# Rotary embedding on one core: the wait for the last ten stores stands at the end of SyncE's program instead of ScalarE's

## The chip, the cores and the metric

The kernel runs on one core of a Trainium2 chip. The metric is the device time of an execution in microseconds (us). The profile's *span* is shorter than this time (160.6 against 162.42 us in the profiled run of before): it ends with the last instruction of the program.

## The reference

A float32 array of 16 x 512 x 1024 is seen as 16 heads of 64 values, and each head is rotated with tables of cosines and sines.

```python
x = x.reshape(batch, seq, num_heads, head_dim)          # 16, 512, 16, 64
x1, x2 = x[..., :half_dim], x[..., half_dim:]
rotated = np.concatenate([x1*cos - x2*sin, x1*sin + x2*cos], axis=-1)
```

The work is light. 33.5 MB have to be read and as many written.

## The kernel before

The kernel is five programs, one for each of five engines. They meet at semaphores, which an instruction or a transfer of one raises (`then_inc`) and another waits for (`wait_ge`). SyncE issues sixteen loads of 2 MB. VectorE multiplies by the cosines, GpSimd (now and then VectorE) multiplies the swapped halves by the signed sines, and the sum of the two is made by VectorE, or by TensorE with an identity matrix and a copy by ScalarE. ScalarE also issues the sixteen stores. Ten loads fit into the ring in SBUF. The last six loads reuse space, so each waits for one of the first six stores, which have semaphores of their own. The last ten stores share one, `sem_rest`.

```python
def on_sync(sp):
    for c in range(NC):                                  # NC = 16
        if c * R >= RING:                                # R = 4, RING = 40
            sp.wait_ge(sem_out[c - RING // R], 16)
        sp.dma_start(tile(c), xv[c]).then_inc(sem_in[c], 16)
        if c == 0:
            ...                                          # loads of the two tables
def on_scalar(ae):
    ...                                                  # copies of the sine table
    for u in range(NU):                                  # NU = 64
        c, r, k = where(u)
        if PE2[u]:
            ae.wait_ge(sem_e, n_pe[u])
            ae.activation(xs[:, k, :], t1_ps[:, u % NT1, :], COPY).then_inc(sem_a, 1)
        if r == R - 1:
            wait_added(ae, u)
            ae.dma_start(ov[c], tile(c)).then_inc(sem_out[c] if c < len(sem_out) else sem_rest, 16)
    ae.wait_ge(sem_rest, 16 * (NC - len(sem_out)))       # the wait in question: 160
```

The last line holds ScalarE until the last ten stores have landed: in before the last of them was issued at 152.16 us and landed at 160.516 us, and the wait ended at 160.555 us.

Of the kernel before, what the change touches and what calls it, by code (L numbers as in the profile page):

```python
# [6 lines left out]
def bass_split_heads_rope_kernel(  # L7
# [29 lines left out]
    NC = batch  # L37
    NU = batch * R

    def where(u):  # L40
        return u // R, u % R, u % RING
# [19 lines left out]
    with ExitStack() as stack:  # L61
# [9 lines left out]
        sem_out = [stack.enter_context(nc.semaphore(f"out{c}")) for c in range(NC - RING // R)]  # L71
        sem_rest = stack.enter_context(nc.semaphore("rest"))
# [21 lines left out]
        def tile(c):  # L94
            k = c * R % RING
            return x_sb[:, k:k + R].rearrange("p n h t d -> p (n h t d)")
# [7 lines left out]
        def wait_added(eng, u):  # L104

            if n_pe[u]:
                eng.wait_ge(sem_a, n_pe[u])
            if n_comb[u]:
                eng.wait_ge(sem_v, n_comb[u])
# [10 lines left out]
        def on_sync(sp):  # L120
            for c in range(NC):
                if c * R >= RING:
# [3 lines that stand above are left out]
                    for i, (table, sem) in enumerate(((cos, sem_cos), (sin, sem_sin))):  # L126
                        sp.dma_start(  # L127
                            stage[:, i, :], table.rearrange("(p r) d -> p (r d)", r=R)
                        ).then_inc(sem, 16)

        def on_scalar(ae):
            ae.wait_ge(sem_sin, 16)
            sv = stage[:, 1, :].rearrange("s (r d) -> s r d", d=HALF)
            ae.activation(s_sb[:, :, 0, :], sv, COPY, scale=-1.0)  # L134
            ae.activation(s_sb[:, :, 1, :], sv, COPY).then_inc(sem_s, 1)  # L135
            for u in range(NU):
# [4 lines that stand above are left out]
                if r == R - 1:  # L141
                    wait_added(ae, u)
                    ae.dma_start(ov[c], tile(c)).then_inc(sem_out[c] if c < len(sem_out) else sem_rest, 16)
            ae.wait_ge(sem_rest, 16 * (NC - len(sem_out)))

        def on_tensor(pe):
            pe.wait_ge(sem_z, 1)
# [49 lines left out]
        def on_vector(ve):  # L197
# [44 lines left out]
            for u in range(NU + LEAD):  # L242
                if u < NU:
                    mul(u)
                if u >= LEAD and not PE2[u - LEAD]:
                    comb(u - LEAD)

        on_sync(nc.sync)
        on_scalar(nc.scalar)
        on_gpsimd(nc.gpsimd)  # L250
        on_tensor(nc.tensor)
# [34 lines left out]
```

## Time and profile before

| before | |
|---|---|
| time, median of 3 runs | 162.3 us (162.14 to 162.39) |
| span of the profiled run, and its time | 160.6 us, 162.42 us |
| last load issued, landed | 84.7 us, 139.3 us |
| last store issued, landed | 152.16 us, 160.52 us |
| the last wait of ScalarE | 160.54 us, 17 ns |

Two lines of the page of before follow: the mean busy share of the 16 DMA engines in 40 equal slices, in tenths, and the rate in each slice.

```profile
DMA  5999999999999999999999999999999999999996
GB/s 147 400 453 425 441 420 400 416 445 416 445 433 416 445 412 447 433 416 441 418 445 433 420 433 429 441 433 420 433 429 437 437 420 437 425 437 441 412 441 286
```

Only the first and the last slice have room. The transfers bound the span, and the stretches of the table view say the same; after the range and its length it gives busy us and number of instructions for PE, PEld, DVE, ACT and POOL, then the granted clock, the DMA share and the rate.

```profile
10.00:50.00 40.00, 20.20 (x28) 6.69 (x28) 36.83 (x33) 6.14 (x6) 40.00 (x18) 0.67 1.01 428
85.00:130.00 45.00, 26.20 (x31) 8.21 (x31) 40.78 (x36) 8.19 (x8) 38.24 (x18) 0.57 1.01 431
156.00:160.60 4.60, 0.00 (x0) 0.00 (x0) 0.00 (x0) 0.00 (x0) 0.00 (x0) 0.50 0.69 296
```

The end, from the view in order of time (start, duration, engine and line), and ScalarE's wait, from the view of its source line:

```profile
151.10 1.02 ACT L140 ACTIVATE x_sb<-t_ps 128x1024 f32<-128x1024 f32 x1 [5.03 <-PE t_ps L164]
152.16 0.34 ACTq L143 DMA_DIRECT2D out_dram<-x_sb  x1
...
L144 ACTq EVENT_SEMAPHORE  x1: 17/17/17, 160.5 to 160.5; - x1
```

After the last copy and the last store's issue no engine computes for 8 us. The wait's record is 17 ns long and begins at 160.538 us, after the last landing at 160.516 us; it holds none of the time from 152.16 us on. A beginner may take the 8 us in front of it for its cost. They are data under way: 360 to 492 GB/s in each microsecond from 152 to 159 us.

### The profile page before, as it was taken

The numbers are of one execution on the slowest core, as the hardware profiler recorded it, in microseconds if no ns is written. First come the engines' busy times: TensorE is split into PE (matmuls) and PEld (weight loads), VectorE is DVE, ScalarE is ACT, GpSimd is POOL, SyncE is SP. The second block draws the span as 40 slices with busy tenths as digits, with TensorE's granted clock in tenths as the row PEclk, the third lists the DMA queues.
The fourth block names the chain that finished last, engine by engine and source line by source line (L and its number), as shares of the span: only waits on it lengthen the run. The fifth ranks groups of instructions, "written<-read, shape, count | busy, mean of one in ns | idle before, by whom it ended". The sixth has DMA issues, their size and how long they took to land.

```text
span 160.6 us, 607 instructions
## 1 busy us (share of the span) xinstructions
PE 84.1 (52%) x102; PEld 26.1 (16%) x102; DVE 131.5 (82%) x116; ACT 26.4 (16%) x27; POOL 130.3 (81%) x62
## 2 busy tenths in 40 slices
PE   6004907363635853864853764764675672684600
PEld 1002301210120220220221120221121121121100
DVE  0089399999999889996999799997999699996800
ACT  3010312022202112112102102202202202202200
POOL 1069999999999999999999993998939989399000
PEclk9955795569655685555675555675555675555775
DMA  5999999999999999999999999999999999999996
GB/s 147 400 453 425 441 420 400 416 445 416 445 433 416 445 412 447 433 416 441 418 445 433 420 433 429 441 433 420 433 429 437 437 420 437 425 437 441 412 441 286
DMA packets 4898, 67.26 MB, mean 419 GB/s; under 512 B 544, under 2 KB 800, under 8 KB 800
## 3 DMA queue, kind: packets, MB, share of 16 engines
q1 hardware_dynamic: 2592, 33.69, 49.9%
q10 hardware_dynamic: 2304, 33.56, 48.8%
q14 instruction: 2, 0.02, 0.0%
HBM read 33.69 MB, written 33.55 MB: 419 GB/s over the span
## 4 chain that ended last, share of the span: by engine, by line
DVE 38%; PE 23%; issue 15%; POOL 7%; ACT 6%; DMA 5%; SPq 0%; DVEq 0%; POOLq 0%
PE t_ps L164 23%; DVE x_sb L235 18%; DVE t_ps L224 16%; POOL t_sb L193 7%; ACT x_sb L140 6%; DVE t_sb L215 5%; DMA stage<-in_sin_dram 5%; SPq L127 0%; SPq L124 0%; ACT s_sb L134 0%; ACT s_sb L135 0%; DVEq L223 0%; DVEq L234 0%; DVEq L221 0%; POOLq L116 0%
## 5 line engine op out<-in xcount | busy, mean ns | idle before, releaser
L193 POOL TENSOR_TENSOR t_sb<-x_sb,s_sb 128x1024 f32<-128x1024 f32 x56 | 129.6, 2364 | 17.7 <-DMA x_sb<-in_x_dram 9.5
L164 PE MATMUL t_ps<-t_sb,ident 128*128 128x512 f32 x96 | 81.4, 999 | 65.7 <-DVE t_ps L224 48.2
L224 DVE TENSOR_TENSOR t_ps<-x_sb,tab_ps 128x1024 f32<-128x1024 f32 x64 | 77.0, 1227 | 12.0 <-ACT x_sb L140 10.3
L235 DVE TENSOR_TENSOR x_sb<-t_ps,t_sb 128x1024 f32<-128x1024 f32 x40 | 48.6, 1218 | 0.0
L164 PEld LDWEIGHTS t_ps<-t_sb,ident 128*128 128x128 f32 x96 | 25.4, 290 | 121.1 <-DVE t_ps L224 87.5
L140 ACT ACTIVATE x_sb<-t_ps 128x1024 f32<-128x1024 f32 x24 | 24.6, 1024 | 118.1 <-PE t_ps L164 118.1
L215 DVE TENSOR_TENSOR t_sb<-x_sb,tab_ps 128x1024 f32<-128x1024 f32 x8 | 9.7, 1211 | 0.0
L202 DVE COPY tab_ps<-stage 128x128 f32<-128x128 f32 x1 | 0.3, 295 | 7.6 <-DMA stage<-in_cos_dram 7.6
L150 PE MATMUL t_ps<-zero 128*128 128x512 bf16 x6 | 2.7, 630 | 1.2 <-DVE zero L198 1.2
L134 ACT ACTIVATE s_sb<-stage 128x128 f32<-128x128 f32 x1 | 0.3, 309 | 6.9 <-DMA stage<-in_sin_dram 6.9
L134 ACT ACT_TABLE_LOAD x1 | 1.3, 1283 | 0.8 <-PEq L268 0.8
L150 PEld LDWEIGHTS t_ps<-zero 128*128 128x128 bf16 x6 | 0.7, 137 | 2.3 <-DVE zero L198 1.2
L198 DVE MEMSET zero<- 128x256 uint32 x1 | 0.3, 272 | 0.9 <-PEq L268 0.9
L175 POOL MEMSET ident<- 128x128 f32 x1 | 0.2, 205 | 0.3 <-POOLq L268 0.3
L177 POOL TENSOR_SCALAR_AFFINE_SELECT ident<-ident 128x128 f32<-128x128 f32 x1 | 0.3, 292 | 0.1
L268 POOL MEMSET const-float32-0.0<- 128x1 f32 x1 | 0.1, 98 | 0.3 <-issue 0.3
L204 DVE TENSOR_SCALAR tab_ps<-stage 128x128 f32<-128x128 f32 x1 | 0.3, 295 | 0.0
L135 ACT ACTIVATE s_sb<-stage 128x128 f32<-128x128 f32 x1 | 0.3, 293 | 0.0
L205 DVE COPY tab_ps<-stage 128x128 f32<-128x128 f32 x1 | 0.3, 284 | 0.0
L268 POOL MEMSET const-bfloat16-1.0<- 128x1 bf16 x1 | 0.1, 101 | 0.0
L268 POOL MEMSET const-uint8-127<- 128x1 uint8 x1 | 0.1, 101 | 0.0
L268 POOL MEMSET const-float32-1.0<- 128x1 f32 x1 | 0.1, 98 | 0.0
## 6 DMA issues: line engine op xcount, KB each, us to landing
x_sb<-in_x_dram SPq DMA_DIRECT2D x16, 2048.0 KB, 54.7
out_dram<-x_sb ACTq DMA_DIRECT2D x16, 2048.0 KB, 18.0
stage<-in_cos_dram SPq DMA_DIRECT2D x1, 64.0 KB, 7.5
stage<-in_sin_dram SPq DMA_DIRECT2D x1, 64.0 KB, 7.2
```

The source lines that it names most:

```text
L134: ae.activation(s_sb[:, :, 0, :], sv, COPY, scale=-1.0)
L135: ae.activation(s_sb[:, :, 1, :], sv, COPY).then_inc(sem_s, 1)
L140: ae.activation(xs[:, k, :], t1_ps[:, u % NT1, :], COPY).then_inc(sem_a, 1)
L150: pe.matmul(t1_ps[:, k, b * BANK:(b + 1) * BANK], zero[:, 0:P], zero[:], start=True, stop=True).then_inc(sem_w, 1)
L164: ins = pe.matmul(t1_ps[:, u % NT1, b * BANK:(b + 1) * BANK], ident[:], t2[:, b * BANK:(b + 1) * BANK], start=False, stop=True, skip_group ...
L177: pl.affine_select(out=ident[:], in_=ident[:], compare_op=mybir.AluOpType.is_equal, fill=0.0, base=0, pattern=[[-1, P]], channel_multiplier=1,
L193: pl.tensor_tensor(t2_sb[:, u % NT2, :, :, :], swapped(k), sin_of(s_sb, r), mult).then_inc(sem_p, 1)
L198: ve.memset(zero[:], 0.0).then_inc(sem_z, 1)
L215: ve.tensor_tensor(t2_sb[:, u % NT2, :, :, :], swapped(k), sin_of(s_ps, r), mult).then_inc(sem_d, 1)
L224: ve.tensor_tensor(t1_ps[:, u % NT1, :].rearrange("p (h d) -> p h d", d=HALF), x_sb[:, k, :, :, :].rearrange("p h t d -> p (h t) d"), c_ps ...
L235: ve.tensor_tensor(xs[:, k, :], t1_ps[:, u % NT1, :], t2_sb[:, u % NT2, :, :, :].rearrange("p h t d -> p (h t d)"), add,).then_inc(sem_v, 1)
L268: nc = _bacc.Bacc("TRN2", target_bir_lowering=False, num_devices=1)
```

## The change

The intent: ScalarE finishes its copies and issues its last store about 8 us before the end, SyncE its last load 76 us before it. If SyncE holds the last wait, ScalarE's program ends early, with its last store's issue (152.5 us in before).

```diff
 def on_sync(sp):
     ...
+            sp.wait_ge(sem_rest, 16 * (NC - len(sem_out)))
 def on_scalar(ae):
     ...
                     ae.dma_start(ov[c], tile(c)).then_inc(sem_out[c] if c < len(sem_out) else sem_rest, 16)
-            ae.wait_ge(sem_rest, 16 * (NC - len(sem_out)))
```

## The prediction

> **What bounds the kernel now.** The transfers. The page's header gives 67.26 MB at a mean of 419 GB/s over a span of 160.6 us, and its slice row shows the 16 DMA engines at 9 tenths or more in all slices but the first and last. The table of stretches gives 428 to 431 GB/s from 10 to 150 us at a DMA share of 1.00. 67.26 MB at 430 GB/s is 156.4 us (estimate from those numbers); the rest is the first fetch and the last landings. VectorE (82%) and GpSimd (81%) are below their limit.

> **The end, the only place the change touches.** In the order of time, ScalarE issues the last store at 152.16 us (0.34 us); from there no engine computes. The stores under way move at 360 to 490 GB/s until 159 us, 82 GB/s in the next microsecond, then nothing. The records of landings show the 160th increment of the shared store semaphore at 160.52 us. ScalarE's wait is one semaphore instruction of 17 ns at 160.54 us, the last of the span. It costs 17 ns and some 20 ns of wake-up; the 8.4 us before it are data.

> **What the change removes, adds and moves.** It removes that instruction from the end of ScalarE's program and adds the same one to the end of SyncE's. SyncE issues its last load at 84.7 us (view of the load line), which lands at 139.3 us, so SyncE stands idle long before 152 us. All sixteen loads are in front of the new wait, and all sixteen stores were in front of the old one, so none is held or released. In the critical tail the same landing releases one 17 ns instruction on another engine: 0.0 us, with 0.05 us either way for a different wake-up.

> **What follows the span.** The time (162.3) is 1.7 us longer than the span. The semaphore records show semaphores being cleared from 161.19 us, 0.65 us after the wait, in blocks of 51, until 161.66 us. [...]

> **Prediction.** 162.3 us, range 161.9 to 162.7 (the three runs of before spread 0.25 us[...]). Faster by over 2% 0.01, within 2% 0.98, slower by over 2% 0.01.

> **What the profile should show.** A span of 160.6 within 0.4 us. The last instruction is a wait of about 17 ns on SyncE, within 0.05 us of the last landing; ScalarE's last is the store issue near 152.2 us. The load queue's six waits on stores stay near 74.7 us in total, all busy times the same within 1%. Clearing still begins about 0.65 us after the last wait.

> **What would make it wrong.** If an engine that ends early could do closing work ahead of the barrier, and ScalarE's were long, the time would fall by up to the 1.7 us outside the span (1%); if SyncE's were longer, it would rise as much. If a waiting SyncE disturbed the transfers from 85 us on, the rate of 430 GB/s would fall. Only that last could pass 2%.

The sum is the 162.3 us of before and 0.0 us, within 0.05, for the moved wait: 162.3 us, as forecast. The spread of 0.25 us and these 0.05 us do not fill the range of 161.9 to 162.7. Two words need their measured meaning. "Cleared" is a reading of the one record that each semaphore from 7 to 255 has behind the last wait of before; by their numbers and times they fall into blocks of 49, 51, 51, 51 and 47. "The barrier": what the runs show of it follows with the semaphore records of the result.

## The result, and the profile after

| | before | after |
|---|---|---|
| time, median of 4 runs | 162.34 us (162.14 to 162.59) | 161.97 us (161.75 to 162.11) |
| span of the profiled run | 160.555 us | 160.531 us |
| last store issued | 152.16 us | 150.47 us |
| last store landed | 160.516 us | 160.497 us |
| end of the last wait to the last record of the execution ("tail") | 2.056 us | 1.603 us |

The ratio is 0.9975, with a 95% interval of 0.9957 to 0.9993. Ratios here are the mean time of one kernel's runs over that of the other's runs of the same rounds, so not quite the ratio of the medians. Executions over 1.5% slower than the fastest of the same kernel are left out of the means.

The same lines of the profile after: from the page, the table of stretches, the order of time, and the view of the new wait's source line. The last line is from the view of the DMA queue's own waits (total us, times, longest).

```profile
DMA  5999999999999999999999999999999999999996
GB/s 151 404 445 429 433 429 404 412 441 421 433 445 416 441 433 418 441 421 437 431 425 441 421 441 425 433 437 420 441 429 429 433 425 441 429 429 437 421 435 290
...
10.00:50.00 40.00, 22.06 (x28) 7.17 (x28) 36.71 (x33) 6.63 (x7) 40.00 (x18) 0.84 1.01 428
85.00:130.00 45.00, 26.59 (x32) 8.34 (x32) 41.39 (x36) 7.35 (x9) 38.90 (x18) 0.62 1.01 431
156.00:160.50 4.50, 0.00 (x0) 0.00 (x0) 0.00 (x0) 0.00 (x0) 0.00 (x0) 0.50 0.73 313
...
150.47 0.34 ACTq L144 DMA_DIRECT2D out_dram<-x_sb  x1
...
L130 SPq EVENT_SEMAPHORE  x1: 17/17/17, 160.5 to 160.5; - x1
...
SPq L130 <- DMA out_dram<-x_sb: 74.0, 1, 74.0
```

The rates are the same (428 and 431 GB/s), and the wait is again 17 ns at the end, now on SyncE. One difference looks like an effect of the change and is not: ScalarE issued the last store 1.69 us earlier. In a repeat of the same kernel, below, the issue came at 153.64 us, later than in before. The granted TensorE clock does not sort these three by itself: it was higher in this execution (mean 0.702 against 0.619), but 0.655 in the late repeat. What moved the issue was not tested. The landing moved by 0.02 us only: in both, the DMA engines were busy with the transfers under way until 159 us (a share of 0.84 to 1.15 in each microsecond from 152 us on).

So the span gave 0.02 us of the 0.4 us. The rest must lie behind the last instruction, where the profile's page shows nothing. The semaphore records of the trace reach further. The kernel's instructions name semaphores from 96 to 134. Of all others, number 2 is the only one with records between 5 us and the last wait, in before and in after. These are all its records from 5 us of the program on, called increments here, in ns from the start of the span:

```
before  last wait ends 160555 (ScalarE)
 151239 | 160969 161008 161051 161074 161172 161212 161246 161293
 162254 162288 162326 162370 162394 162492 162530 162564 162611
after   last wait ends 160531 (SyncE)
 148919 151078 151116 151159 | 160652 160696 160734 160769 160815
 161776 161810 161849 161893 161916 162014 162053 162087 162134
```

The bar marks the last wait. Each execution has two groups of nine increments. In before, one increment comes before the wait and eight of the first group after it. In after, four come early and five are left. This leads to Theory A, a guess from these counts: the group is a barrier, a point at which each engine waits for the others; each engine has its place in the row of increments and takes its turn when the one before it has taken its own, and the late engine's place in that row, with its own time to get there, decides what is left after the last wait. The records do not say which engine made an increment.

Behind the last wait the semaphores from 7 to 255 have one record each, in before at 161.189 to 161.858 us; in after 232 of the 249 are recorded, at 160.768 to 161.380 us. They are read as the clearing of the semaphores.

The parts of the two tails, in us:

| part of the tail | before | after | difference |
|---|---|---|---|
| end of the wait to the late engine's own increment | 0.414 | 0.121 | -0.293 |
| rest of the first group | 0.324 (7 steps) | 0.163 (4 steps) | -0.161 |
| first group's last to second group's first (most of the clearing of semaphores lies here; it begins 0.05 to 0.10 us before the first group's last) | 0.961 | 0.961 | 0.000 |
| second group | 0.357 | 0.358 | 0.001 |
| sum | 2.056 | 1.603 | -0.453 |

The 0.161 us of the second row is not steps alone: the three that came early in after took 0.105 us in before, and nearly all the rest is one step, the one behind SyncE's increment, which took 0.098 us in before and 0.044 us in after.

The measured time appears to end with this tail: in both profiled runs it is 0.19 us short of the last increment (162.42 against 162.611, and 161.94 against 162.134), and so it is, by 0.189 to 0.201 us, in all twelve profiles but one. The tail's 0.453 us and the span's 0.024 us add up to 0.477, and the two times differ by 0.48 us.

### The profile page after: what moved, and what is told of

Its sections match the earlier page's. It is cut to its first block, busy times and chain, and to the rows that moved or that the text cites. A ratio compares the mean times of both kernels' runs of the same rounds, so it can differ in the third digit from the quotient of the medians.

```text
span 160.5 us, 607 instructions
## 1 busy us (share of the span) xinstructions
PE 81.7 (51%) x102; PEld 25.4 (16%) x102; DVE 131.5 (82%) x116; ACT 26.3 (16%) x27; POOL 130.3 (81%) x62
## 4 chain that ended last, share of the span: by engine, by line
DVE 36%; PE 19%; issue 17%; POOL 10%; ACT 5%; DMA 5%; SPq 0%; DVEq 0%; POOLq 0%
PE t_ps L164 19%; DVE x_sb L235 18%; DVE t_ps L224 15%; POOL t_sb L193 10%; ACT x_sb L141 5%; DMA stage<-in_sin_dram 5%; DVE t_sb L215 4%; SPq L127 0%; SPq L124 0%; ACT s_sb L135 0%; ACT s_sb L136 0%; DVEq L234 0%; DVEq L223 0%; POOLq L116 0%; DVEq L221 0%
## 5 line engine op out<-in xcount | busy, mean ns | idle before, releaser
L164 PE MATMUL t_ps<-t_sb,ident 128*128 128x512 f32 x96 | 78.9, 972 | 65.8 <-DVE t_ps L224 49.8
L164 PEld LDWEIGHTS t_ps<-t_sb,ident 128*128 128x128 f32 x96 | 24.7, 281 | 119.4 <-DVE t_ps L224 86.4
```

Of the source, the lines that this page charges most:

```text
L164: ins = pe.matmul(t1_ps[:, u % NT1, b * BANK:(b + 1) * BANK], ident[:], t2[:, b * BANK:(b + 1) * BANK], start=False, stop=True, skip_group ...
```

## The experiments

Rivals of Theory A were: the gain is chance in the span (N); ScalarE gains because it is free to close early, whoever holds the wait (F); something about a waiting SyncE (S). The compared kernels ran on one chip, with their own runs of before.

### Moving the wait to each engine in turn

First the kernel after once more, as the control.

> The kernel after, unchanged, as the control of this call. 'Tail' is the time from the end of the last wait to the last increment of semaphore 2 in the records; it was 2.06 us before and 1.60 us after. Theory A (late engine's place in the closing barrier): tail 1.60 us within 0.05, nine increments in the first group of which five come after the wait, ratio to before 0.997 to 0.998, time less span near 1.42 us. Rival N (the 0.4 us was chance in the span): the ratio's interval has 1.000 well inside.

Measured: 162.12 us (162.02 to 162.27, 5 runs) against 162.53 us for 11 runs of before; ratio 0.9977, interval 0.9965 to 0.9989. Tail 1.605 us, with five of the first nine increments after the wait. Over all these runs the mean of time less span went from 1.88 to 1.41 us (-0.47), while the mean span went from 160.61 to 160.72 us, the wrong way. Rival N falls.

In the next three kernels the line is deleted from SyncE's program and stands at the end of another engine's.

```diff
-            sp.wait_ge(sem_rest, 16 * (NC - len(sem_out)))
# at the end of on_tensor, on_vector or on_gpsimd
+            pe.wait_ge(sem_rest, 16 * (NC - len(sem_out)))      # or ve., or pl.
```

> The last wait stands at the end of TensorE's program, ScalarE and SyncE are both free early. Theory A, with TensorE first in the order of increments (the lone increment 0.17 us after its last matmul in both traces): all nine increments of the first group come after the wait; tail = 0.17 to 0.41 us of TensorE's own + 8 x 0.041 to 0.046 + 1.32 = 1.83 to 2.10 us, so time like before or up to 0.25 us under it. Rival F (what gained was that ScalarE was free to close early): tail 1.60 us and time 161.97, like after.

> The last wait stands at the end of VectorE's program. Theory A: VectorE is third or fourth in the order, so six or seven increments of the first group come after the wait, tail = own 0.12 to 0.41 + 5 or 6 x 0.041 to 0.046 + 1.32 = 1.65 to 2.0 us; time between after and before, or near before. Rival F: tail 1.60 us, five increments after the wait, time like after.

> The last wait stands at the end of GpSimd's program. Theory A: GpSimd is the other of third and fourth: seven or six increments after the wait (one more or one fewer than with VectorE), tail 1.65 to 2.0 us. Rival F: tail 1.60 us, five increments after the wait, time like after.

The results, with before and after beside them. "Early" is how many of the first nine increments came before the last wait; "own" and "rest" are the first two parts of the tail; time less span is the mean of the timed runs. The parts of the tail in the row of before are those of its first profile.

| wait on | early | own | rest, steps | tail | time less span | time, median | ratio to before (interval) |
|---|---|---|---|---|---|---|---|
| TensorE | 0 | 0.187 | 0.485, 8 | 2.090 | 2.22 | 162.81 | 1.0028 (1.0004 to 1.0052) |
| ScalarE (before) | 1 | 0.414 | 0.324, 7 | 2.056 | 1.88 | 162.53 | 1 |
| GpSimd | 2 | 0.533 | 0.284, 6 | 2.137 | 1.94 | 162.68 | 1.0007 (0.9995 to 1.0019) |
| VectorE | 3 | 0.147 | 0.242, 5 | 1.709 | 1.51 | 162.17 | 0.9984 (0.9972 to 0.9996) |
| SyncE (control) | 4 | 0.123 | 0.162, 4 | 1.605 | 1.41 | 162.12 | 0.9977 (0.9965 to 0.9989) |

TensorE is not fully explained. In its only profile one of its eight steps took 0.160 us instead of the 0.034 us seen at that place with other engines, the gap to the second group was 1.061 us instead of 0.961 us, and its time was 163.39 us in the profiled run, 0.64 us *after* the last increment and not 0.19 us before it. Its six runs spread from 162.32 to 163.80 us, with spans of 160.4 to 161.1 us. In four of them the time less span is 1.89 to 1.93 us, which is what the tail of 2.090 us less 0.19 us gives. In the other two, the profiled one among them, it is 2.69 and 3.00 us. So the tail fits four runs, and two have about 0.8 to 1.1 us more; in the profiled one that lies behind the last increment. Without these two the mean is 162.64 us against 162.49 us for before, so "slower than before" rests on them. What the extra time is stays open.

### Both engines hold the wait

```diff
 # after, with the old line put back as well
+            ae.wait_ge(sem_rest, 16 * (NC - len(sem_out)))
```

> Both ScalarE and SyncE hold the last wait. Theory A: ScalarE's turn comes before SyncE's, so this ends like before: eight increments of the first group after the wait, tail 2.06 us within 0.06, time like before (ratio 0.999 to 1.001). If it was SyncE being held that shortened the ending (a rival S: something about SyncE waiting), tail 1.60 us and ratio 0.9975.

Measured: 162.48 us (162.32 to 162.51) against 162.45 us, ratio 0.9999, interval 0.9985 to 1.0013. One early increment, own 0.416 us, tail 2.053 us. ScalarE's turn decides although SyncE waits as well. Rival S falls. The gain came from what was taken off ScalarE, as long as it isn't put on an engine that leaves as long a tail, as GpSimd (2.137 us) and TensorE (2.090 us) do.

### Why ScalarE takes 0.41 us to its turn

Four kernels with one run each, whose state is unknown, were made to explain the own time. The readings from them are of their traces, not of their times.

> After, with ScalarE's program ended by a wait on the first store, long landed. It asks why ScalarE took 0.414 us from its last wait to its own increment in before, but 0.271 us from the end of its last store's issue in after. If that is because a program that ends with a semaphore wait takes longer to leave, ScalarE's increment comes 0.40 us after its last instruction; if it is because ScalarE had been blocked for 8 us, it comes 0.27 us after or sooner. Tail 1.60 us and time like after either way.

```diff
 # at the end of on_scalar of after
+            ae.wait_ge(sem_out[0], 16)
```

Measured: ScalarE's increment came 0.514 us after that wait. Both alternatives of the expectation were wrong. The tail was 1.604 us and the time 162.11 us.

> After, with five waits on long landed stores at the end of ScalarE's program instead of none. ScalarE is off the critical path, so tail 1.60 us. Its own increment: 0.51 us after the last of the five if an unheld wait costs that, 0.27 us if the 0.51 us of the run with one such wait still held work of the store's issue in front of it, which five waits leave time for.

```diff
 # at the end of on_scalar of after
+            for c in range(5):
+                ae.wait_ge(sem_out[c], 16)
```

Measured: 0.165 us after the last of the waits, which is neither value again. The five waits had become three instructions, and between the second and the third lay 0.347 us in which nothing is recorded. The tail was 1.602 us and the time 162.09 us.

> Before, with one more wait on ScalarE behind the last one, on a store long landed. So far ScalarE's increment came 0.41 us after its wait when it had been held there (before, both held) and 0.51 us after an unheld wait. If the way from a program's end to the increment is fixed work after the last instruction, the increment comes 0.41 to 0.42 us after the end of the second wait. If it is counted from the moment of release, with the extra wait hidden in it, it comes 0.41 us after the first wait and under 0.38 us after the second. If an unheld wait at the end costs 0.51 us, as in the run before, 0.51 us after the second. The first group has eight increments after the waits in each case; tail from the last wait 1.98 to 2.16 us.

```diff
 # before
             ae.wait_ge(sem_rest, 16 * (NC - len(sem_out)))
+            ae.wait_ge(sem_out[0], 16)
```

> After, with one more wait behind the last on SyncE, on a store long landed. Theory A: the increments after it are the same five; SyncE's own comes 0.12 us after the second wait (0.15 at most), so tail from the end of the last wait is 1.60 us within 0.03, and the time is longer by the second wait alone, 0.02 to 0.06 us. If SyncE too pays more for an unheld wait at its end (0.1 us on ScalarE), its increment comes 0.2 us or more after.

```diff
 # after
             sp.wait_ge(sem_rest, 16 * (NC - len(sem_out)))
+            sp.wait_ge(sem_out[0], 16)
```

These two did not test what they were made for, because each pair of waits was compiled into one instruction with two conditions. They serve as repeats of before and after: own 0.415 us, tail 2.055 us, time 162.71 us; own 0.122 us, tail 1.604 us, time 161.75 us. Their records also teach caution. The wait with two conditions is recorded as 9461 ns long on ScalarE, from 151.389 us on, and 75,092 ns on SyncE, where the wait with one condition is recorded as 17 ns.

So ScalarE's own time is repeatable when it is held (0.414, 0.416 and 0.415 us), but it varied from 0.165 to 0.514 us after its last instruction in other endings. What fills it stays open.

### A try at the span

The wait has now stood on each of the five engines, so no other place of it is to be tried. What remains is the span. After moved only 98 GB/s from 2 to 3 us and 328 GB/s from 3 to 4 us, and I asked whether the table loads were in the way of the second load.

```diff
 # after: the two table loads are issued by ScalarE, ahead of all its work
-                        sp.dma_start(stage[:, i, :], ...)
+                ae.dma_start(stage[:, i, :], ...)
```

> After, with the two table loads issued by ScalarE's queue, so that SyncE's second load of x is issued near 1.2 us instead of 2.17 us. It asks whether the span itself, which the change left alone, has room at its start: the stretch from 2 to 4 us moved only 98 and 328 GB/s. If that hole was the late issue of the second load, the span falls by up to 1 us, to about 159.7, and the time to about 161.2 (ratio to before 0.992 to 0.995). If the hole is made by the 512-byte pieces of the tables on the engines, wherever they are issued, the time stays that of after (ratio 0.997 to 0.998). Tail 1.60 us either way.

Measured: 164.58 us (162.64 to 167.26, 7 runs, of which three are slow); ratio of the fast runs 1.0089, interval 1.0072 to 1.0107. It was a miss in the other direction. The three have no lower clock (0.643 to 0.664) than the other four (0.609 to 0.697), so their length may belong to this kernel. The tail was 1.605 us as expected, but the span grew. The table loads of the page (size, us from issue to landing) and the start of the work in order of time show a part of how, first after, and under it the start of GpSimd's work in before:

```profile
stage<-in_sin_dram SPq DMA_DIRECT2D x1, 64.0 KB, 7.2
...
9.56 11.58 POOL L193 TENSOR_TENSOR t_sb<-x_sb,s_sb 128x1024 f32<-128x1024 f32 x5 [8.19 <-ACT s_sb L135]
```

Then the try:

```profile
stage<-in_sin_dram ACTq DMA_DIRECT2D x1, 64.0 KB, 12.7
...
13.94 0.31 ACT L134 ACTIVATE s_sb<-stage 128x128 f32<-128x128 f32 x1 [10.93 <-DMA stage<-in_sin_dram]
...
14.53 2.34 POOL L192 TENSOR_TENSOR t_sb<-x_sb,s_sb 128x1024 f32<-128x1024 f32 x1 [13.15 <-ACT s_sb L135]
```

From its own queue the sine table took 12.7 us instead of 7.2 us to land, so GpSimd began its multiplications at 14.5 us; in before they began at 9.56 us and in after at 9.54 us. GpSimd and VectorE are busy for 81 and 82% of the span, so little is there to absorb a start 5 us late. That this delay makes all of the longer span was not tested, and it can't be seen here for the slower runs: the profile is of the fastest of the seven (span 161.2 us), and the others have spans of 162.4 to 165.8 us. The second load was issued at 1.23 us instead of 2.17 us, and the hole at 2 to 4 us stayed (116 and 303 GB/s), so the late issue of that load did not make it alone.

## Why the prediction was right, and where it was not

- **The transfers bound the span, and the change does not touch them: right.** 428 and 431 GB/s in both, and a last store issued 1.69 us earlier landed only 0.02 us earlier.
- **In the span the change is worth 0.0 us within 0.05: right.** The wait is one 17 ns instruction in both and begins about 20 ns after the last landing. That the two spans differ by only 0.024 us shows less than it seems to, as the spans of after alone run from 160.3 to 160.9 us.
- **The time, 162.3 us in 161.9 to 162.7: 161.97 us, inside but near the low edge.** That is in part luck: the tail lost 0.453 us, more than the 0.4 us from the prediction to its low edge, and one of the four runs (161.75 us) lies below it. "Within 2%" holds.
- **The mis-sized term is what follows the span.** The prediction's estimate of it, with the sign open, was smaller than what was measured. The first group's rest took 0.161 us less. The estimate left out the late engine's own time to its turn, 0.414 us on ScalarE and 0.121 us on SyncE, worth 0.293 us. Together the tail lost 0.453 us.
- **"Clearing still begins about 0.65 us after the last wait": wrong.** It was 0.634 us before and 0.237 us after; in after the records lie within 0.61 us (0.237 to 0.849 us after the wait). The prediction also ends the clearing of before too early: at 161.66 us four of the five blocks are done, and the last record lies at 161.86 us.
- **The first clause under "what would make it wrong" came near.** ScalarE did take longer from its last wait to its turn in the barrier (0.414 us) than SyncE (0.121 us), and when ScalarE ended early its increment came early as well (at 151.08 us in after). What fills the time remains open.
- **"All busy times the same within 1%": wrong for TensorE** (84.1 and 81.7 us, at mean clocks of 0.619 and 0.702; its weight loads 26.1 and 25.4 us). The load queue's six waits came to 76.1 us instead of "near 74.7". Neither shows in the last landing.

## What to carry to other kernels

In this program the last wait stood best on the engine whose turn in the closing barrier comes last (four early increments) and that gets there fastest (0.12 us). That is SyncE, and it was worth about 0.45 us of tail against ScalarE and 0.53 us against GpSimd. No other program was tried. If the amount is the same there, it weighs most in short programs, so look there first. Here the wait after the last data cost its 17 ns and its engine's way to its turn (0.12 us on SyncE to 0.53 us on GpSimd), not the 8 us in front of it. When two kernels have the same span and different times, look at what is recorded behind the last instruction before you look for a cause in the work.
